# Decoder step on one core: the samples' outputs from the old recurrent state, the state's update moved behind the branches

## The chip, the core and the metric

The kernel runs on one core of a Trainium2 chip. The core has a matrix engine (TensorE, PE in the profile, with its weight loads as PEld), a vector engine (VectorE, DVE), a scalar engine (ScalarE, ACT), GpSimd (POOL) and SyncE (SP). Each takes its instructions in the order of its own queue and waits for others by semaphores. Transfers between the main memory and the on-chip memory are issued by SP, POOL and ACT and run on 16 DMA engines. TensorE writes into PSUM, a small accumulator memory that VectorE and ScalarE read.

The metric is the time of one execution on the device, in microseconds (us); less is better.

## What is computed

One layer of a decoder for a prompt of 256 tokens and, beside it, 8 samples with one new token each. The input projection feeds three parallel branches (a spatial gating, an HGRN2 recurrence with 8 heads of 128 x 128 state, a GLA recurrence with 4 heads of 128 x 256 state); their outputs are merged by gates, projected, and an MLP (2048 to 8192 and back) follows. All is in 32-bit floats. The part that matters here is the recurrence:

```python
"""S_t = diag(f_t) S_{t-1} + k_t v_t^T ; o_t = S_t^T q_t (per head)."""
o = einsum('bhts,bshv->bthv', att, vc) + einsum('bthd,bhdv->bthv', qc * exp(b), S)
S = exp(b_last)[..., None] * S + einsum('bshd,bshv->bhdv', kc * exp(b_last[:, None] - b), vc)
```

For a sample there is one step only: from the given state S, the decay f, the key k, the value v and the query q come the new state S' = diag(f) S + k vᵀ, which is an output of the kernel, and the output o = S'ᵀ q. The same output can be written with the old state: o = Sᵀ (f · q) + v (k · q).

## The kernel before

**The stream.** 256 prompt tokens and 8 samples stand together as 264 columns. Each weight block of 128 x 128 is split into a high part (`whi`, a cast on ScalarE, L109) and the rest (`wlo`, a subtraction on VectorE, L106), and each product takes three matmuls (L601 to L603) in which the columns pass. `granule` runs 24 such matmuls on a 512 KB piece of weights. `Stream` loads the pieces through SP into four `raw` buffers and splits them two pieces ahead, into six pairs of `whi` and `wlo`.

**Phases.** First the main input projection, in chunks; then the branch phase: `gla_group`, then for each of the three branches the gates' projection (`zin`) and the branch's own (`linear` with `w_branch`); then `w_out`; then the MLP in eight blocks, `up` of a block before `down` of the one ahead.

**Background work.** The branches' small work is written as generators. After each granule `background()` counts a tick (`now[0]`) and pumps two queues: `bg` (the mixers: transposes, decay levels, attention within the prompt) and `bs` (the samples' states), each with a rate per tick. `yield x` costs x of the rate, `yield READY` holds until the next tick, `yield` of a condition holds until it is true. `slot()` puts the small matmuls that have become ripe (levels, samples, the adaLN products of `Rounds`) into the stream, when something is due or has waited for some ticks.

**Who sets the order.** In the branch phase the order on PE and POOL is the program's own (`manual_schedule`), in the MLP phase that on PE alone. The instructions of the other engines are put in order by the framework's scheduler, which takes data and buffers into account; tiles with one name (`st`, `vbc`, `vt` and so on) share a fixed number of buffers.

**The samples' states before.** There are three groups: HGRN heads 0 to 3, heads 4 to 7 (state 128 x 128 a head), and GLA (128 x 256 a head). `mixer_r` brings the samples' values to rows and writes them to memory (`vs_d`, L1130); when the gates are done, `samples_r` (L1058) goes to `bs`. In 8 steps (16 for GLA) of one sample and 128 x 512 elements of state it loads the state into `st` (L1073, POOL) and the values, the same for all partitions, into `vbc` (L1079, POOL); multiplies by the decay on ScalarE (L1099, one instruction a head); adds value times key on VectorE (L1101); writes the new state out (L1102, POOL) and hands `st` to `samples`. `slot()` multiplies it with the query, masked so that each sample has its row (`qm`, L640), and VectorE adds the products to `os_` (L647, L103). At the end `os_` is normalised (L1111 to L1113), and `finish` (L1300) transposes it into the branch's columns. `st` has four buffers, `vbc` two; a further state is fetched only while at most one state is handed over and unread.

```python
for i in range(nh):
    S.activation(st[:, i, :], st[:, i, :], AF.Copy, scale=fs[:, h0 + i, b:b + 1])
for i in range(nh):
    V.scalar_tensor_tensor(st[:, i, :], v[:, i, :], k[:, h0 + i, NP + b:NP + b + 1], st[:, i, :], ALU.mult, ALU.add)
nc.gpsimd.dma_start(G.s_out(b, h0, nh), st)
```

Other lines that are spoken of: `srow` (L862, L865), the samples' rows in `sample_rows`; `G2`, a product of two vectors for the last norm, emitted ahead of the last `down`; the loads of `x_prompt` (L1406) behind the branches; L1220, the attention between the prompt's two halves, which needs `kd`; L1340 and L1342, the gating of a branch's product.

Of the kernel before, what the change touches and what calls it, by code (L numbers as in the profile page):

```python
# [10 lines left out]
AF = mybir.ActivationFunctionType  # L11
ALU = mybir.AluOpType
# [3 lines left out]
P = 128  # L16
D = 2048
KT = D // P
NP = 256
NS = 8  # L20
NT = NP + NS
# [16 lines left out]
ST_BUFS = 4  # L38
VB_BUFS = 2
# [8 lines left out]
READY = object()  # L48
SLOT_WAIT = 4
HELD_OWED = 1.0  # L50
LEVELS_HELD = 3
FETCHED = 3
AGE = 2
ADA_LAND = 4

# [2 lines left out]
def hybrid_step_kernel(  # L58
# [8 lines left out]
    nc = tc.nc  # L67
    V, S, T = nc.vector, nc.scalar, nc.tensor
# [29 lines left out]

    def mul(o, a, b):
        V.tensor_tensor(o, a, b, op=ALU.mult)  # L100

    def add(o, a, b):
        V.tensor_tensor(o, a, b, op=ALU.add)  # L103
# [14 lines left out]
    ident, ones, triu = cst[:, 0:128], cst[:, 128:256], cst[:, 256:384]  # L118
    rmask, delta = cst[:, 384:648], cst[:, 648:904]
# [29 lines left out]
    ps = sm()  # L149
# [205 lines left out]
    now = [0]  # L355
# [41 lines left out]
    bg, bs = Queue(), Queue()  # L397
# [98 lines left out]
    rate = [0.0, 0.0]  # L496
# [110 lines left out]
    levels, samples = [], []  # L607

    def slot():

        lv = [x for x in levels if x[0] + AGE <= now[0]][:2]
        if any(x[3] == 64 for x in lv):
            lv = lv[:1]
        sv = [x for x in samples if x[0] + AGE <= now[0]]
        del levels[:len(lv)]
        del samples[:len(sv)]
        pls, two = [], None
        for _, lhs, rhs, m, _ in lv:
            if m == 64:
                pl = sm([P, 8, 64])  # L620
            else:
                two = two or sm([P, 2, 8, 32])
                pl = two[:, len(pls)]
            pls.append(pl)
            n = max(m, 32)
            for h in range(4):
                for hf in range(2):
                    for b in range(4):
                        if m >= 32 and b // (n // 32) % 2:
                            continue  # L630
                        t0 = hf * P + b * 32
                        q0 = t0 if m < 32 else hf * P + b // (n // 32) * n + n
                        T.matmul(pl[32 * b:32 * b + 32, 2 * h + hf, :], lhs[:, h, t0:t0 + 32], rhs[:, h, q0:q0 + n], start=True, stop=True)  # L633
        if sv:
            G, qm, os_ = sv[0][1]
            nh = 512 // G.dv
            po = sm([P, G.dv])
            for h in range(4):
                for i, (_, _, b, sts) in enumerate(sv):
                    T.matmul(po[32 * h:32 * h + 32, :], qm[:, h, b, :], sts[h // nh][:, h % nh, :], start=i == 0, stop=i == len(sv) - 1)  # L640
        if rounds.due():
            rounds.steps()
        for pl, x in zip(pls, lv):
            x[4](pl)
        if sv:
            if sv[0][2] == 0:
                V.tensor_copy(os_, po)  # L647
            else:
                add(os_, os_, po)

    later = []

# [222 lines left out]
    def mixer_a():  # L875
# [6 lines left out]
        for gg in range(2):  # L882
            ps = sm()
# [5 lines left out]
        ps = sm()  # L889
# [3 lines left out]
        for v in vtk:  # L893
            st = tmp([P, 2, 6], "bst", 1)
# [11 lines left out]
            add(v, v, lnb)  # L906
            yield

        vs = tmp([P, 8, NS], "vsa", 1)
        w8 = tmp([P, 8, NS], "vsb", 1)  # L910
        r8 = tmp([P, NS], "vsr", 1)
        for i in range(2):
# [4 lines left out]
        ps = sum_partitions(w8, NS)  # L917
# [7 lines left out]
        ps = sum_partitions(w8, NS)  # L925
# [9 lines left out]
        ps = sm([P, P])  # L935
# [11 lines left out]
        for gp in range(4):  # L947
            ps = sm()
# [30 lines left out]

    att = const([P, 8, P], "att")  # L980
    nc.gpsimd.memset(att, 0.0)
    vs_d = dp.tile([3, 8 * NS, P], F32, tag="vs_d", name="vs_d")

    class Group:
# [73 lines left out]
    def samples_r(G):  # L1058

        dv = G.dv  # L1060
        nj, nh = dv // P, 512 // dv
        q, k, g = G.q, G.k, G.g
        fs = tmp([P, 4, NS], "fs")
        S.activation(fs, g[:, :, NP:NT], AF.Exp)
        qm = blk([P, 4, NS, 32])
        mul(qm, q[:, :, NP:NT].unsqueeze(3).to_broadcast([P, 4, NS, 32]),
            delta.rearrange("p (b c) -> p b c", b=NS).unsqueeze(1).to_broadcast([P, 4, NS, 32]))
        steps = [(b, h) for b in range(NS) for h in range(0, 4, nh)]
        ahead, vals = [], []

        def fetch(b, h):
            st = tmp([P, nh, dv], "st", ST_BUFS)
            nc.gpsimd.dma_start(st, G.s_in(b, h, nh))  # L1073
            ahead.append((st, now[0]))

        def values(b, h):
            v = tmp([P, 4, P], "vbc", VB_BUFS)
            r0 = 4 * nj * b + h * nj
            nc.gpsimd.dma_start(v, vs_d[G.i, r0:r0 + 4, :].partition_broadcast(P))  # L1079
            vals.append((v.rearrange("p (h j) v -> p h (j v)", h=nh), now[0]))  # L1080

        for s in steps[0:2]:
            fetch(*s)
            yield
        values(*steps[0])
        yield
        os_ = tmp([P, dv], f"os{G.i}", 1)
        sts = []
        for n, (b, h0) in enumerate(steps):
            if n + 2 < len(steps):  # L1090

                yield lambda: len(sts) + sum(len(x[3]) for x in samples) <= ST_BUFS - 3
                fetch(*steps[n + 2])
            if n + 1 < len(steps):
                values(*steps[n + 1])
            yield lambda: now[0] >= max(ahead[0][1] + FETCHED, vals[0][1] + FETCHED - 1)
            st, v = ahead.pop(0)[0], vals.pop(0)[0]
            for i in range(nh):
                S.activation(st[:, i, :], st[:, i, :], AF.Copy, scale=fs[:, h0 + i, b:b + 1])  # L1099
            for i in range(nh):  # L1100
                V.scalar_tensor_tensor(st[:, i, :], v[:, i, :], k[:, h0 + i, NP + b:NP + b + 1], st[:, i, :], ALU.mult, ALU.add)  # L1101
            nc.gpsimd.dma_start(G.s_out(b, h0, nh), st)  # L1102
            sts.append(st)
            if h0 + nh == 4:
                samples.append((now[0], (G, qm, os_), b, sts))
                sts = []
            yield
        yield lambda: not samples
        yield READY
        ss, rr = tmp([P, 1], "sss", 1), tmp([P, 1], "srr", 1)  # L1110
        S.activation(tmp([P, dv], "vt"), os_, AF.Square, accum_out=ss)  # L1111
        rstd_small(ss, 1.0 / dv, rr)
        S.activation(os_, os_, AF.Copy, scale=rr)  # L1113
        G.os = os_
        yield

    def mixer_r(G):
# [172 lines left out]
                yield 0.6  # L1290
        G.o = o

    def finish(i):
        bg.drain(gens[i])
        G = Gs[i]
        while not hasattr(G, "os"):
            bs.drain(bs.g[0])
        for j in range(G.dv // P):
            ps = sm([P, P])
            T.transpose(ps, G.os[:, j * P:(j + 1) * P], ident)  # L1300
            V.tensor_copy(G.o[j][:, :, NP:NT], ps.rearrange("p (h c) -> p h c", h=4)[:, :, 0:NS])

    gens, Gs = [], []
# [101 lines left out]
        for hf in range(2):  # L1405
            nc.gpsimd.dma_start(x1[t][hf], x_prompt[0, t * P:(t + 1) * P, hf * 1024:(hf + 1) * 1024])  # L1406
    sqacc = tmp([P, NT], "a32", 1)
    gs = tmp([P, KT, NS], "gs", 1)

    def gated(m, src, Gv):  # L1410

# [62 lines left out]
    for m in range(7):  # L1474
        if m in PRE_AT:
            n = N_PRE // len(PRE_AT)
# [77 lines left out]
    ps = sm([P, 2, 14, NS])  # L1554
# [16 lines left out]
    ps = sm([P, 2 + NS])  # L1571
# [35 lines left out]
    q = tmp([P, 2 + NS], "rr", 1)  # L1607
# [116 lines left out]
    def up(f, zs=()):  # L1724
        ah, al = [], []
        for m in range(FB // CW):
            z = zs[m] if m < len(zs) else linear(w_mlp_up[0], 0, KT, f * FB + m * CW, CW, h2H, h2L)
            rl = tmp([P, 2, NT], "vt")
            S.activation(rl, z, AF.Relu)  # L1729
            if m % 2 == 0:  # L1730
                ah.append(blk(dt=F32R))
                al.append(blk(dt=F32R))
            a, b = pair(ah[-1], m % 2), pair(al[-1], m % 2)
            sq = tmp([P, 2, NT], "gt")
            S.activation(a, rl, AF.Square)  # L1735
            mul(sq, rl, rl)
            sub(b, sq, a.bitcast(F32))
        return tiles(ah), tiles(al)
# [31 lines left out]
    order = tc.manual_schedule(engines={mybir.EngineType.PE})  # L1770
    order.__enter__()
    pend = up(0, zs)
    for f in range(NFB):
        nxt = up(f + 1) if f + 1 < NFB else None
        if f == NFB - 1:
            rounds.drain()
            mul(G2, mod[:, 5 * KT:6 * KT, :], gpost2T.unsqueeze(2).to_broadcast([P, KT, NC]))
            yt = [[blk([P, 1024]) for _ in range(2)] for _ in range(2)]
        g = down(f, *pend)
        pend = nxt  # L1780
# [89 lines left out]
```

## Time and profile before

| What | Value |
|---|---|
| Median of 3 runs | 1937.15 us (1937.14 to 1942.04) |
| Profiled execution | 1936.48 us |
| Its span in the trace | 1934.7 us |
| TensorE busy | 1900.5 us |
| VectorE busy | 1191.7 us |
| ScalarE busy | 996.9 us |
| DMA traffic | 442.06 MB, 228 GB/s on the mean |
| Loads of states (`st`) | 32 of 256 KB |
| Loads of values (`vbc`) | 32 of 256 KB |
| Writes of states | 32 of 256 KB |

Line numbers (L1101) are those of the kernel before. A group's row gives line, engine and operation, what it writes and reads, the shapes and the count, then its busy time, the mean length of one in ns, and the idle time of its engine just ahead of it with what ended most of that. A row of a timeline gives start, length, engine, line and operation, and in brackets the idle time ahead and its releaser. A row of windows gives a stretch, its length, the busy time of PE, PEld, DVE, ACT and POOL (with instructions), then the clock that TensorE was granted, the share of the DMA engines in use and GB/s. A row that begins with a line and has "min/median/max" in ns gives also the first and last start in us.

### The profile page before, as it was taken

How to read it: one execution, taken by the hardware profiler on the slowest of the kernel's cores; microseconds unless marked ns; L12 is line 12 of the kernel's file. 1: busy time of each engine (PE TensorE's matmuls, PEld its weight loads, DVE VectorE, ACT ScalarE, POOL GpSimd, SP SyncE). 2: the span in 40 equal slices, each digit the busy share in tenths (PEclk: the TensorE clock that was granted, in tenths of full speed). 3: DMA queues.
4: the chain of work that ended last, by engine and by line, in shares of the span. 5: the costliest groups of instructions: out<-in, count | busy, mean ns of one | idle time of the engine just before them, and what ended most of it. 6: DMA issues, size and time to landing. Idle time of an engine off the chain costs nothing.

```text
span 1934.7 us, 42322 instructions
## 1 busy us (share of the span) xinstructions
PE 1900.5 (98%) x17092; PEld 1811.2 (94%) x17092; DVE 1191.7 (62%) x2129; ACT 996.9 (52%) x1812; POOL 87.7 (5%) x144
## 2 busy tenths in 40 slices
PE   7999999998999999999999999999999999999998
PEld 5989999998999998999999999999999999999997
DVE  5666567685577695565555667545555555555666
ACT  4444354664666765544444566454444545454544
POOL 1000000001101112200000010000000000000000
PEclk9999999999999999999999999999999999999999
DMA  9986696777588678987777846776655556565563
GB/s 325 349 319 236 226 307 206 226 254 252 184 269 278 221 260 277 309 264 251 251 252 231 304 143 193 230 239 188 183 178 183 182 179 184 176 184 179 181 183 102
DMA packets 339380, 442.06 MB, mean 228 GB/s; under 512 B 14930, under 2 KB 281024, under 8 KB 339184
## 3 DMA queue, kind: packets, MB, share of 16 engines
q1 hardware_dynamic: 329120, 409.62, 65.6%
q0 software_dynamic: 8992, 28.48, 4.6%
q8 instruction: 134, 2.20, 0.4%
q10 hardware_dynamic: 1072, 1.25, 0.2%
q14 instruction: 62, 0.51, 0.1%
HBM read 427.60 MB, written 11.70 MB: 227 GB/s over the span
## 4 chain that ended last, share of the span: by engine, by line
PE 94%; DVE 2%; DMA 2%; ACT 1%; issue 1%; POOL 0%; SPq 0%; DVEq 0%; ACTq 0%
PE mm L601 29%; PE mm L602 28%; PE mm L603 28%; PE ada L341 3%; PE ada L273 2%; DMA vbc<-vs_d 1%; PE sm L633 1%; DVE wlo L106 1%; PE sm L845 1%; PE sm L640 0%; DMA st<-in_state_gla_dram 0%; DMA b<-in_x_prompt_dram 0%; DVE b L103 0%; DMA b<-in_w_ada_dram 0%; ACT b L109 0%
## 5 line engine op out<-in xcount | busy, mean ns | idle before, releaser
L601 PE MATMUL mm<-b,whi 128*128 128x264 f32 x4592 | 1318.1, 287 | 5.7 <-DVE b L103 2.9
L602 PE MATMUL mm<-b,whi 128*128 128x264 f32 x4592 | 1307.7, 285 | 1.4 <-DVE b L106 1.2
L603 PE MATMUL mm<-b,wlo 128*128 128x264 f32 x4592 | 1305.1, 284 | 3.1 <-DVE wlo L106 2.6
L106 DVE TENSOR_TENSOR wlo<-raw,whi 128x512 fp32r<-128x512 f32 x1136 | 770.3, 689 | 498.0 <-ACT whi L109 495.4
L109 ACT CAST whi<-raw 128x512 fp32r<-128x512 f32 x1132 | 692.3, 618 | 726.9 <-PE mm L602 648.2
L601 PEld LDWEIGHTS mm<-b,whi 128*128 128x128 f32 x4592 | 865.4, 188 | 49.2 <-issue 24.7
L603 PEld LDWEIGHTS mm<-b,wlo 128*128 128x128 f32 x4592 | 865.5, 188 | 3.7 <-DVE wlo L106 3.7
L602 PEld LDWEIGHTS mm<-b,whi 128*128 128x128 f32 x4592 | 865.5, 188 | 2.4 <-DVE b L106 1.3
L103 DVE TENSOR_TENSOR b<-b,mm 128x528 f32<-128x528 f32 (+1 forms) x137 | 95.7, 700 | 98.2 <-PE mm L603 98.2
L1101 DVE SCALAR_TENSOR_TENSOR st<-vbc,b,st 128x128 f32<-128x128 f32 (+1 forms) x96 | 34.2, 391 | 54.7 <-DMA vbc<-vs_d 49.8
L1099 ACT ACTIVATE st<-st,fs 128x128 f32<-128x128 f32 (+1 forms) x96 | 37.0, 430 | 58.7 <-DMA st<-in_state_hgrn_dram 32.5
L273 PE MATMUL ada<-b,cT 128*32 128x256 f32 (+1 forms) x640 | 34.7, 354 | 6.9 <-DMA b<-in_w_ada_dram 6.8
L341 PE MATMUL ada<-araw,cT 128*32 128x512 f32 x296 | 39.9, 601 | 0.0
L273 PEld LDWEIGHTS ada<-b,cT 128*32 128x32 f32 x640 | 17.8, 112 | 18.8 <-ACT b L234 6.1
L100 DVE TENSOR_TENSOR b<-b,b 128x512 f32<-128x512 f32 (+1 forms) x47 | 34.1, 742 | 1.4 <-ACT b L1209 0.9
L1102 POOL DMA_DIRECT2D out_dram<-st x32 | 23.5, 735 | 156.4 <-DVE st L1101 155.6
L341 PE MATMUL ada<-b,cT 128*32 128x512 f32 x216 | 25.8, 593 | 0.0
L106 DVE TENSOR_TENSOR b<-gt,b 128x528 fp32r<-128x528 f32 x32 | 22.7, 708 | 3.6 <-ACT whi L109 0.5
L106 DVE TENSOR_TENSOR b<-b 128x1024 f32<-128x1024 f32 (+1 forms) x24 | 24.3, 1018 | 0.0
L100 DVE TENSOR_TENSOR gt<-vt 128x528 f32<-128x528 f32 x32 | 22.5, 702 | 0.9 <-ACT vt L1729 0.9
L1735 ACT ACTIVATE b<-vt 128x528 fp32r<-128x528 f32 x32 | 20.7, 647 | 1.0
L341 PEld LDWEIGHTS ada<-b,cT 128*32 128x32 f32 x216 | 6.9, 110 | 15.1 <-issue 14.6
(385 smaller groups left out, 882.6 us busy)
## 6 DMA issues: line engine op xcount, KB each, us to landing
raw<-in_w_in_dram SPq DMA_DIRECT2D x232, 512.0 KB, 4.6
raw<-in_w_mlp_up_dram SPq DMA_DIRECT2D x128, 512.0 KB, 3.7
raw<-in_w_mlp_down_dram SPq DMA_DIRECT2D x128, 512.0 KB, 3.6
b<-in_w_ada_dram SPq DMA_DIRECT2D x102, 512.0 KB, 6.3
araw<-in_w_ada_dram SPq DMA_DIRECT2D x74, 512.0 KB, 5.4
raw<-in_w_branch_dram SPq DMA_DIRECT2D x48, 512.0 KB, 4.3
raw<-in_w_out_dram SPq DMA_DIRECT2D x32, 512.0 KB, 4.2
b<-in_w_ada_dram SPq DMA_DIRECT2D x32, 256.0 KB, 6.5
```

Source lines behind the costliest of these rows:

```text
L100: V.tensor_tensor(o, a, b, op=ALU.mult)
L103: V.tensor_tensor(o, a, b, op=ALU.add)
L106: V.tensor_tensor(o, a, b, op=ALU.subtract)
L109: S.copy(hi, src)
L273: T.matmul(acc[32 * j:32 * j + 32, 0:n], cT[:, k, :], w[:, n * j:n * j + n], start=k == 0, stop=k == KT - 1)
L341: T.matmul(self.acc[32 * j:32 * j + 32, :], cT[:, k, :], ws[j // 2][:, j % 2 * 512:j % 2 * 512 + 512], start=k == 0, stop=k == KT - 1)
L601: T.matmul(o, a, xh(k + j), start=first and j == 0, stop=False)
L602: T.matmul(o, a, xl(k + j), start=False, stop=False)
L603: T.matmul(o, b, xh(k + j), start=False, stop=last and j == n - 1)
L1099: S.activation(st[:, i, :], st[:, i, :], AF.Copy, scale=fs[:, h0 + i, b:b + 1])
L1101: V.scalar_tensor_tensor(st[:, i, :], v[:, i, :], k[:, h0 + i, NP + b:NP + b + 1], st[:, i, :], ALU.mult, ALU.add)
L1102: nc.gpsimd.dma_start(G.s_out(b, h0, nh), st)
```

## The change

In `samples_r` the state is not updated any more. The old state is loaded and handed to `slot()` as it is; the masked query is multiplied by the decay first (`qf`). The second term, value times (key · query), goes into `os_` ahead of the products: the samples' values are copied to a padded tile, transposed by PE (one transpose for a group of HGRN, two for GLA), and scaled by key · query, for which PE multiplies `pads` (by then k times q) with a column of ones. Loads now alternate over six buffers (every third takes a `vbc` buffer), and up to three states may wait for PE. Decay and key of each group are kept in a new tile, `kept`.

A new generator, `states()`, goes to `bs` when the first block of `up` has been issued, at a rate of 0.4 a tick. It walks over all 32 steps, loads state and values again, and does the multiplication on ScalarE, the addition on VectorE and the write that `samples_r` did. The names of three small tiles change so that they share buffers.

```diff
-FETCHED = 3
+FETCHED = 4
+UPDATE_RATE = 0.4
...
-            if sv[0][2] == 0:
-                V.tensor_copy(os_, po)
-            else:
-                add(os_, os_, po)
+            add(os_, os_, po)
...
+    kept = const([P, 3, 2, 4 * NS], "kept")
...
-        fs = tmp([P, 4, NS], "fs")
+        fs, ks = (kept[:, G.i, c].rearrange("p (h b) -> p h b", h=4) for c in range(2))
         S.activation(fs, g[:, :, NP:NT], AF.Exp)
+        V.tensor_copy(ks, k[:, :, NP:NT])
+        yield
...
         def fetch(b, h):
-            st = tmp([P, nh, dv], "st", ST_BUFS)
+            odd = fetched[0] % 3 == 2
+            fetched[0] += 1
+            st = tmp([P, nh, dv], "vbc" if odd else "st", VB_BUFS if odd else ST_BUFS)
             nc.gpsimd.dma_start(st, G.s_in(b, h, nh))
...
+        pads = tmp([P, 4, 32], "xsn", 1)
+        nc.gpsimd.memset(pads, 0.0)
+        for j in range(nj):
+            for i, b in enumerate(G.v):
+                V.tensor_copy(pads[:, i * nh:(i + 1) * nh, 0:NS], b[:, j::nj, NP:NT])
+            yield READY
+            yield READY
+            ps = sm([P, P])
+            T.transpose(ps, pads.rearrange("p h b -> p (h b)"), ident)
+            S.copy(os_[:, j * P:(j + 1) * P], ps)
+            yield
+        qf = tmp([P, 4, NS], "fs")
+        mul(pads[:, :, 0:NS], q[:, :, NP:NT], ks)
+        mul(qf, q[:, :, NP:NT], fs)
         yield
...
+        yield READY
+        ps = sm([P, 8])
+        T.matmul(ps[:, 0:1], pads.rearrange("p h b -> p (h b)"), ones[:, 0:1], start=True, stop=True)
+        kq = tmp([P, 1], "sss", 1)
+        V.tensor_copy(kq, ps[:, 0:1])
+        yield
+        S.activation(os_, os_, AF.Copy, scale=kq)
+        yield
...
-                yield lambda: len(sts) + sum(len(x[3]) for x in samples) <= ST_BUFS - 3
+                yield lambda: len(sts) + sum(len(x[3]) for x in samples) <= ST_BUFS - 1
                 fetch(*steps[n + 2])
...
-            for i in range(nh):
-                S.activation(st[:, i, :], st[:, i, :], AF.Copy, scale=fs[:, h0 + i, b:b + 1])
-            for i in range(nh):
-                V.scalar_tensor_tensor(st[:, i, :], v[:, i, :], k[:, h0 + i, NP + b:NP + b + 1], st[:, i, :], ALU.mult, ALU.add)
-            nc.gpsimd.dma_start(G.s_out(b, h0, nh), st)
-            sts.append(st)
+            yield lambda: now[0] >= ahead[0][1] + FETCHED
+            sts.append(ahead.pop(0)[0])
...
-            yield
+            yield 0.5
...
+    def states():
+
+        todo = [(G, b, h) for G in Gs for b in range(NS) for h in range(0, 4, 512 // G.dv)]
+        ahead = []
+
+        def fetch(G, b, h):
+            nj, nh = G.dv // P, 512 // G.dv
+            st, v = tmp([P, nh, G.dv], "st", ST_BUFS), tmp([P, 4, P], "vbc", VB_BUFS)
+            nc.gpsimd.dma_start(st, G.s_in(b, h, nh))
+            r0 = 4 * nj * b + h * nj
+            nc.gpsimd.dma_start(v, vs_d[G.i, r0:r0 + 4, :].partition_broadcast(P))
+            ahead.append((st, v.rearrange("p (h j) v -> p h (j v)", h=nh), now[0]))
+
+        fetch(*todo[0])
+        yield
+        for n, (G, b, h) in enumerate(todo):
+            if n + 1 < len(todo):
+                fetch(*todo[n + 1])
+                yield 0.5
+            yield lambda: now[0] >= ahead[0][2] + FETCHED
+            st, v = ahead.pop(0)[0:2]
+            nh = 512 // G.dv
+            for i in range(nh):
+                f, k = (kept[:, G.i, c, (h + i) * NS + b:(h + i) * NS + b + 1] for c in range(2))
+                S.activation(st[:, i, :], st[:, i, :], AF.Copy, scale=f)
+                V.scalar_tensor_tensor(st[:, i, :], v[:, i, :], k, st[:, i, :], ALU.mult, ALU.add)
+                if i % 2:
+                    yield 0.5
+            nc.gpsimd.dma_start(G.s_out(b, h, nh), st)
+            yield
...
     pend = up(0, zs)
+    bs.g.append(states())
+    rate[:] = (0.0, UPDATE_RATE)
...
             rounds.drain()
+            assert not bs.g
```

More of the change, by code (lines that the diff above doesn't have):

```diff
@@ L907, in mixer_a @@
             yield
-        vs = tmp([P, 8, NS], "vsa", 1)
+        vs = tmp([P, 8, NS], "os1", 1)
         w8 = tmp([P, 8, NS], "vsb", 1)
@@ L1062, in samples_r @@
         q, k, g = G.q, G.k, G.g
-        fs = tmp([P, 4, NS], "fs")
+        fs, ks = (kept[:, G.i, c].rearrange("p (h b) -> p h b", h=4) for c in range(2))
         S.activation(fs, g[:, :, NP:NT], AF.Exp)
-        qm = blk([P, 4, NS, 32])
-        mul(qm, q[:, :, NP:NT].unsqueeze(3).to_broadcast([P, 4, NS, 32]),
-            delta.rearrange("p (b c) -> p b c", b=NS).unsqueeze(1).to_broadcast([P, 4, NS, 32]))
+        V.tensor_copy(ks, k[:, :, NP:NT])
+        yield
         steps = [(b, h) for b in range(NS) for h in range(0, 4, nh)]
-        ahead, vals = [], []
+        ahead, fetched = [], [0]
@@ L1071, in fetch @@
         def fetch(b, h):
-            st = tmp([P, nh, dv], "st", ST_BUFS)
+            odd = fetched[0] % 3 == 2
+            fetched[0] += 1
+            st = tmp([P, nh, dv], "vbc" if odd else "st", VB_BUFS if odd else ST_BUFS)
             nc.gpsimd.dma_start(st, G.s_in(b, h, nh))
             ahead.append((st, now[0]))
[L1076 to L1080, printed above, removed]
@@ L1082, in samples_r @@
         for s in steps[0:2]:
             fetch(*s)
+        os_ = tmp([P, dv], f"os{G.i}", 1)
+        pads = tmp([P, 4, 32], "xsn", 1)
[8 more added lines that the diff above has]
+            S.copy(os_[:, j * P:(j + 1) * P], ps)
@@ L1084, in samples_r @@
             yield
-        values(*steps[0])
+        qf = tmp([P, 4, NS], "fs")
+        mul(pads[:, :, 0:NS], q[:, :, NP:NT], ks)
+        mul(qf, q[:, :, NP:NT], fs)
         yield
-        os_ = tmp([P, dv], f"os{G.i}", 1)
+        qm = blk([P, 4, NS, 32])
+        mul(qm, qf.unsqueeze(3).to_broadcast([P, 4, NS, 32]),
+            delta.rearrange("p (b c) -> p b c", b=NS).unsqueeze(1).to_broadcast([P, 4, NS, 32]))
+        yield READY
+        ps = sm([P, 8])
+        T.matmul(ps[:, 0:1], pads.rearrange("p h b -> p (h b)"), ones[:, 0:1], start=True, stop=True)
@@ L1090, in samples_r @@
             if n + 2 < len(steps):
-                yield lambda: len(sts) + sum(len(x[3]) for x in samples) <= ST_BUFS - 3
+                yield lambda: len(sts) + sum(len(x[3]) for x in samples) <= ST_BUFS - 1
                 fetch(*steps[n + 2])
[L1094 to L1097, printed above, removed]
-            for i in range(nh):
-                S.activation(st[:, i, :], st[:, i, :], AF.Copy, scale=fs[:, h0 + i, b:b + 1])
-            for i in range(nh):
-                V.scalar_tensor_tensor(st[:, i, :], v[:, i, :], k[:, h0 + i, NP + b:NP + b + 1], st[:, i, :], ALU.mult, ALU.add)
-            nc.gpsimd.dma_start(G.s_out(b, h0, nh), st)
-            sts.append(st)
+            yield lambda: now[0] >= ahead[0][1] + FETCHED
+            sts.append(ahead.pop(0)[0])
             if h0 + nh == 4:
@@ L1407, in hybrid_step_kernel @@
     sqacc = tmp([P, NT], "a32", 1)
-    gs = tmp([P, KT, NS], "gs", 1)
+    gs = tmp([P, KT, NS], "os0", 1)
     def gated(m, src, Gv):
```

## The prediction

> **What bounds the kernel now.** I read the page's head, the chain, what TensorE (PE) waits for, and then the windows.
>
> ```profile
> span 1934.7 us, 42322 instructions
> PE 1900.5 (98%) x17092; PEld 1811.2 (94%) x17092; DVE 1191.7 (62%) x2129; ACT 996.9 (52%) x1812; POOL 87.7 (5%) x144
> PE 94%; DVE 2%; DMA 2%; ACT 1%; issue 1%; POOL 0%; SPq 0%; DVEq 0%; ACTq 0%
> ```
>
> PE is busy 98% of the span and 94% of the chain is PE. Only two things can move the time: PE's own work, and the places where PE stands. Between 320 and 520 us PE's waits are these two (us in total, times, longest), in the 350 us that follow only the next two:
>
> ```profile
> PE sm L1220 <- DVE b L100: 3.8, 1, 3.8
> PE mm L603 <- DVE wlo L106: 1.9, 1, 1.9
> ...
> PE mm L603 <- issue: 0.5, 1, 0.5
> PE mm L603 <- DVE wlo L106: 0.2, 1, 0.2
> ```
>
> The timelines of VectorE (DVE) and PE (start, length; in brackets the idle time before and its releaser) show where they come from:
>
> ```profile
> 454.92 0.61 DVE L1101 SCALAR_TENSOR_TENSOR st<-vbc,b,st 128x128 f32<-128x128 f32 x2 [7.71 <-DMA vbc<-vs_d]
> 456.81 0.39 PE L603 MATMUL mm<-b,wlo 128*128 128x264 f32 x1 [1.91 <-DVE wlo L106]
> 471.51 0.88 DVE L1101 SCALAR_TENSOR_TENSOR st<-vbc,b,st 128x128 f32<-128x128 f32 x3 [1.26 <-DMA vbc<-vs_d]
> 477.75 0.49 PE L1220 MATMUL sm<-b,b 128*128 128x128 f32 x2 [3.84 <-DVE b L100]
> ```
>
> DVE works in queue order. At 447 us the state update (L1101) is at its head and waits 7.71 us for the broadcast values, `vbc`; the weight halves `wlo` behind it come late, and PE stands 1.91 us. Its backlog, with more update instructions and another wait, makes `kd` late at 477 us: 3.84 us. Both gaps are followed by matmuls at about half the clock (window, its length, busy PE, PEld, DVE, ACT, POOL; granted clock, DMA share, GB/s):
>
> ```profile
> 458.00:462.00 4.00, 3.97 (x20) 3.67 (x19) 3.71 (x7) 3.46 (x10) 0.00 (x0) 0.57 0.55 141
> 478.00:482.00 4.00, 4.00 (x23) 4.00 (x23) 0.30 (x1) 1.14 (x2) 0.00 (x0) 0.59 0.93 300
> ```
>
> That costs 4 x 0.43 = 1.7 and 4 x 0.41 = 1.6 us. Updates of the samples' states thus hold PE up by 1.9 + 3.8 + 1.7 + 1.6 = **9.1 us**, all in group 0.
>
> The Trainium skill's page "TensorE: Matmul & The Clock Gate" (What's actually happening) has the clock halve after at least one idle window of about 3.4 us; here a gap of 1.91 us was enough. By the page the first gap would cost 1.9 us and the gain would be 7.4 us; the windows decide for 9.1.
>
> **The change, part by part.**
>
> *The update leaves the branch phase.* PE no longer waits for ScalarE (ACT), DVE or `vbc`; it reads the old state as it lands. A slot comes at least 4 + 2 background ticks after the fetch is emitted; a tick is 24 matmuls. With 2305 matmuls in 280 us (a window quoted below) that is 2.9 us, so 17 us against a landing of 11.3 at most (next rows). I put PE's wait for these loads at nothing. Both stalls go: -9.1. The least that I allow is -5, if the chain to L1220 stays late for other reasons; the most is -9.8, with the 0.5 and 0.2 above.
>
> *New PE work*: 4 transposes of the samples' values and 3 products with a column of ones, in some 7 visits. The nearest rows are a visit with two transposes:
>
> ```profile
> 668.65 0.28 PE L603 MATMUL mm<-b,wlo 128*128 128x264 f32 x1
> 668.77 0.38 PE L1300 MATMUL sm<-cst,os 128*128 128x128 f32 x2
> 668.91 0.37 PE L601 MATMUL mm<-b,whi 128*128 128x264 f32 x1
> 669.11 0.28 PE L602 MATMUL mm<-b,whi 128*128 128x264 f32 x1
> ```
>
> From L603 to L602 are 0.46 us, where two steps of the stream (0.12 each, 668.65 to 668.77) take 0.24: 0.22 a visit, 7 x 0.22 = **+1.5 us** (0.7 if visits fall together, 3 if each stands alone). The small copies and products on DVE and ACT replace 32 updates there, and the new memset on POOL stands behind two fetches that POOL issues well ahead; I cost them at nothing. Should POOL be late, DVE waits about 2 us, which the update's longer waits without a PE stall (below) show to be covered.
>
> *The update elsewhere*: 32 steps, each with a second load of the state, the broadcast `vbc`, 96 ACT and 96 DVE instructions in all, and the write. The issue times on POOL, in ns (min/median/max), and the landings:
>
> ```profile
> L1099 ACT ACTIVATE st<-st,fs 128x128 f32<-128x128 f32 (+1 forms) x96 | 37.0, 430 | 58.7 <-DMA st<-in_state_hgrn_dram 32.5
> L1101 DVE SCALAR_TENSOR_TENSOR st<-vbc,b,st 128x128 f32<-128x128 f32 (+1 forms) x96 | 34.2, 391 | 54.7 <-DMA vbc<-vs_d 49.8
> L1102 POOL DMA_DIRECT2D out_dram<-st x32: 712/742/764, 404.7 to 836.6; - x32
> L1073 POOL DMA_DIRECT2D st<-in_state_gla_dram x16: 707/722/732, 665.5 to 821.7; - x16
> L1079 POOL DMA_DIRECT2D vbc<-vs_d x32: 549/562/809, 374.7 to 830.8; - x32
> DMA to landing us min/median/max: 3.7/6.5/11.3
> ```
>
> A step costs 34.2/32 = 1.07 us of DVE, 37.0/32 = 1.16 of ACT and 0.74 + 0.72 + 0.56 = 2.0 of POOL. Spread over the MLP phase (0.4 a tick, 2 to 2.5 a step: one step in 5 to 6 ticks, 16 us) this would cost nothing: DVE is at 164/280 = 58% there, DMA at 0.60.
>
> ```profile
> 1600.00:1880.00 280.00, 280.00 (x2305) 280.00 (x2305) 163.62 (x244) 132.59 (x218) 0.00 (x0) 1.00 0.60 181
> ```
>
> **But will it be spread?** In that phase only PE's order is fixed by hand. What the scheduler does with instructions of other engines can be read from early starters:
>
> ```profile
> L100 DVE TENSOR_TENSOR G<-mod,vec x2: 302/304/306, 559.5 to 1340.6; 128x144 f32<-128x144 f32 x2
> L1419 DVE TENSOR_SCALAR gt<-b,G x8: 347/348/354, 1877.7 to 1921.3; 128x256 f32<-128x256 f32 x8
> L862 DVE COPY srow<-b x4: 190/192/200, 346.1 to 530.5; 128x32 f32<-128x32 f32 x4
> L865 PE MATMUL sm<-cst,srow x3: 271/272/272, 369.0 to 662.8; 128*128 128x128 f32 x3
> L1406 POOL DMA_DIRECT2D b<-in_x_prompt_dram x4: 528/546/569, 1011.6 to 1029.5; - x4
> L1342 DVE SCALAR_TENSOR_TENSOR gt<-gt,mm x16: 693/704/705, 689.3 to 1046.3; 128x528 f32<-128x528 f32 x16
> ```
>
> The product for `G2` is emitted ahead of the last `down` block, a few us before its first use at 1877.7; it ran at 1340.6, when its input was there. The copies into `srow` are emitted just before their transposes (662.8 the last); the last ran at 530.5. Both went up, by 130 and 530 us, to their data. The loads of `x_prompt` came early too, but not at the start: their tiles took their turn in the pool. The pacing by ticks fixes PE's order alone. `states()` hands PE nothing, so its loads start when the `st` tiles, in their turn, come free after the last samples' matmuls, and each step then follows as fast as two `vbc` buffers allow:
>
> ```profile
> L640 PE MATMUL sm<-st,b x192: 269/279/404, 424.9 to 845.3; 128*32 128x128 f32 x128, 128*32 128x256 f32 x64
> 802.63 0.72 POOL L1073 DMA_DIRECT2D st<-in_state_gla_dram x1 [8.07 <-PE sm L640]
> 801.68 0.62 ACT L109 CAST whi<-raw 128x512 fp32r<-128x512 f32 x1 [0.84 <-PE mm L602]
> 809.14 0.91 ACT L1099 ACTIVATE st<-st,fs 128x256 f32<-128x256 f32 x2 [6.83 <-DMA st<-in_state_gla_dram]
> 40.00:100.00 60.00, 60.00 (x647) 54.99 (x646) 38.45 (x66) 25.85 (x44) 0.00 (x0) 1.00 0.97 342
> 840.00:1050.00 210.00, 210.00 (x1734) 198.32 (x1733) 116.68 (x186) 95.16 (x154) 2.18 (x4) 1.00 0.77 251
> ```
>
> So I expect the 32 updates from about 845 us, beside the third branch. The load issued at 802.63 landed at 809.1, yet its consumer stands in ACT's queue right behind the cast of 801.68, one cast (1.5 us) later than the slot: the order counts on loads that land in about 2 us. The order is therefore as dense as the engines allow: DVE is idle 1 - 117/210 = 44% there, so a step takes 1.07/0.44 = 2.4 us of planned time, in which PE does 2.4 us of work. On the chip a step takes longer. By latency, two in flight: (2.0 + 6.5 + 1.07)/2 = 4.8 us with the median landing, 3.4 with the shortest. By traffic: three transfers of 0.262 MB plus PE's weights for 2.4 us at 251 GB/s (0.60 MB) make 1.39 MB, at the 342 GB/s of a stretch with DMA at 0.97: 4.1 us. I take 4.1, between the latency ends. PE loses (4.1 - 2.4) x 32 = 54 us, less one cover of about 7 us (the 6.83 us wait above brought no PE stall worth naming): **+47 us**. The ends: 3.4 gives 32 - 7 = 25, 4.8 gives 77 - 7 = 70.
>
> The sum: the profiled execution took 1936.48 us, 1.8 above its span and 0.7 below the median of the runs. 1936.5 - 9.1 + 1.5 + 47 = 1975.9; with the 0.7, 1976.6, say **1976**.
>
> **Rivals.**
>
> *A, the update does stay in the MLP phase.* If tiles of one pool are handed out in program order whatever their name, the `st` tiles wait their turn behind the `vt` and `gt` tiles of `up`, which PE paces. For it: the turn that the `x_prompt` tiles took. Against it: those share one name with what held them, and tiles of another pool did not hold them: they came before the last accumulator ahead of them was read (L1342, 1046.3). Then 1937.2 - 9.1 + 1.5 = 1929.6, **faster**. It decides as soon as a step takes over 4.8 us of planned time, the time of one by latency: all landings are then hidden.
>
> *B, dense, but landings are short.* The shortest landing of a state load was 3.0 us:
>
> ```profile
> DMA to landing us min/median/max: 3.0/5.7/11.3
> ```
>
> A step then takes (2.0 + 3.0 + 1.07)/2 = 3.0 us, PE loses 0.6 x 32 - 7 = 12, and the time is 1942 (1932 to 1955). For it: a standing PE asks for fewer weights. Against it: medians of 5.7 and 6.5 at spacings wider than here. The Trainium skill's page "DMA: Bandwidth & Descriptors" (Anatomy of one DMA, SWDGE path) fits 2.0 us plus bytes over 436 GB/s, 2.6 us for such a load; by that, an estimate, the step takes 2.8 us and 6 us are lost after the cover, 1936. No landing of these loads in the trace was that short.
>
> *C, the stalls are replaced*: spread or not, a new wait in the branch phase (a transpose or product whose copy on DVE or ACT is late) takes back what L1220 gives. One such gap with its slow clock is 3.8 + 1.6 = 5.4 us: 1935. For it: three groups, seven new points where PE needs something from DVE. Against it: ready-waits of one or two ticks ahead of each.
>
> *D, spread, but DVE waits for `vbc` in the MLP phase.* `down` frees an accumulator every two granules, 5.8 us, so waits over about 6 us stall PE, at 1.9 + 1.7 to 3.8 + 1.6 us each: with four of them 1929.6 + 18 = 1948. Against it: DMA at 0.60 and 16 us between steps.
>
> **How the numbers follow.** Forecast (dense, 1955 to 2007) 0.47; A 0.25; B 0.12; C 0.09; D 0.07. About 0.3% (5.8 us) is what a measurement can tell from no change. Faster: A's 0.22 and 0.02 of B and C, 0.24. Same: A 0.03, B 0.04, C 0.07, D 0.02, in all 0.16. Slower: 0.60. The range goes from A's 1928 to 2005, where the upper latency end (1976.6 + 70 - 47 = 2000) and some slow clock behind the gaps lie; below and above it about 0.15 are left out. The forecast's own range is 1955 to 2005.
>
> **What would show it.** Dense: the update's ACT and DVE lines start near 845 us and end before 1000; DVE waits there for `vbc` tens of us in total; PE waits for `wlo` and `whi`, its busy share falls, and DMA rises above 0.9 in these slices. Spread: the same lines run from about 1200 to 1740 us and PE has no gap there. In either case the gaps at 455 and 474 us are gone, no L1101-like line stands before 800 us, and PE has 7 short visits more. I am wrong if the update starts late, or if it starts at 845 us and PE still does not stand; and in the branch part, if PE waits for `st` loads.

## The result and the profile after

The kernel after the change takes 1995.0 us (median of 5 runs, 1994.37 to 1996.86), the one before 1937.15 us on the same chip (5 runs): ratio 1.030, 95% interval [1.029, 1.031]. It is slower by 58 us, where the forecast was 1976 us in a range of 1928 to 2005. The profiled execution took 1996.86 us, 2.1 us above its span.

The page of the kernel after: its head, then TensorE's (PE's) busy time and granted clock in 40 slices of 50 us, and the share of each engine in the chain that ended last.

```profile
span 1994.8 us, 42421 instructions
PE 1922.0 (96%) x17102; PEld 1826.6 (92%) x17102; DVE 1198.8 (60%) x2143; ACT 1001.0 (50%) x1819; POOL 111.3 (6%) x179
PE   7999999999999999876899999999999999999998
...
PEclk9999999999999999988999999999999999999999
...
PE 80%; issue 9%; DMA 6%; DVE 2%; POOL 1%; ACT 1%; SPq 0%; DVEq 0%; ACTq 0%; POOLq 0%
```

PE's share of the chain fell from 94% to 80%. Its busy digits drop in slices 17 to 20, 800 to 1000 us, its clock in two of these; elsewhere only the first and the last slice are below 9. PE is busy for 21.5 us more than before with ten instructions more: a part of the loss is PE itself running slower. The rows of the `st` tiles say what runs in those slices (ns min/median/max, first and last start in us):

```profile
L1326 ACT ACTIVATE st<-st,kept x96: 384/398/512, 803.1 to 964.9; 128x128 f32<-128x128 f32 x64, 128x256 f32<-128x256 f32 x32
L1327 DVE SCALAR_TENSOR_TENSOR st<-vbc,kept,st x96: 343/348/485, 804.3 to 979.0; 128x128 f32<-128x128 f32 x64, 128x256 f32<-128x256 f32 x32
```

So all 32 steps of the update, emitted in the MLP phase, ran at 803 to 979 us, 5.5 us a step, beside the third branch. What the engines waited for between 785 and 990 us (us in total, times, longest): PE, then VectorE (DVE), ScalarE (ACT) and GpSimd (POOL):

```profile
PE mm L604 <- DVE wlo L107: 22.7, 17, 4.8
PE mm L602 <- ACT whi L110: 19.1, 8, 9.6
PE mm L602 <- ACT gt L1373: 2.4, 2, 2.0
...
DVE wlo L107 <- ACT whi L110: 39.2, 23, 5.0
DVE st L1327 <- DMA vbc<-vs_d: 33.0, 10, 5.5
...
ACT st L1326 <- DMA st<-in_state_hgrn_dram: 30.8, 7, 8.3
ACT st L1326 <- DMA st<-in_state_gla_dram: 23.4, 8, 6.7
...
POOL st L1310 <- DMA out_dram<-st: 57.6, 24, 5.9
```

An ACT or DVE that stands for a load of the update has the casts and subtractions of the weight stream behind it; PE then has no `whi` or `wlo`. PE's three lines add up to 44.2 us. The windows (length; busy PE, PEld, DVE, ACT, POOL with instructions; granted clock, DMA share, GB/s), first over the whole stretch, then its worst part, then the places of the two old stalls; below them the first and the last of these stretches in the kernel before:

```profile
785.00:985.00 200.00, 155.57 (x1094) 140.78 (x1093) 100.38 (x219) 89.23 (x201) 64.59 (x96) 0.88 0.86 277
...
920.00:960.00 40.00, 23.95 (x146) 22.78 (x145) 19.80 (x40) 16.82 (x33) 15.24 (x23) 0.74 0.90 301
...
455.00:482.00 27.00, 27.00 (x300) 25.68 (x299) 15.39 (x32) 13.35 (x25) 0.00 (x0) 1.00 0.63 184
```

```profile
785.00:985.00 200.00, 199.79 (x1657) 187.01 (x1653) 111.58 (x192) 95.53 (x168) 13.97 (x21) 1.00 0.83 271
...
455.00:482.00 27.00, 21.33 (x185) 19.83 (x186) 20.58 (x41) 14.57 (x31) 4.84 (x7) 0.88 0.82 263
```

In 200 us PE stood for 44.4 us, and the clock of 0.88 took another 0.12 x 200 = 24 us: 68 us lost. The count of matmuls says the same: 1094 where the kernel before ran 1657, and 563 at 200/1657 = 0.121 us are 68 us. The two stalls of before are gone (27.00 of 27 us busy at full clock), which gave back 5.7 us of idle time and 0.12 x 27 = 3.2 us of clock, less the time of the new PE work. With some 8 us for that, 68 - 8 = 60 is the difference of the spans (1994.8 - 1934.7).

### The profile page after: what moved, and what is told of

Same layout as the page of the kernel before. It is cut to its first block, busy times and chain, and to the rows that moved or that the text cites. A ratio compares the mean times of both kernels' runs of the same rounds, so it can differ in the third digit from the quotient of the medians.

```text
span 1994.8 us, 42421 instructions
## 1 busy us (share of the span) xinstructions
PE 1922.0 (96%) x17102; PEld 1826.6 (92%) x17102; DVE 1198.8 (60%) x2143; ACT 1001.0 (50%) x1819; POOL 111.3 (6%) x179
## 4 chain that ended last, share of the span: by engine, by line
PE 80%; issue 9%; DMA 6%; DVE 2%; POOL 1%; ACT 1%; SPq 0%; DVEq 0%; ACTq 0%; POOLq 0%
PE mm L602 24%; PE mm L603 24%; PE mm L604 24%; DMA out_dram<-st 3%; PE ada L342 2%; PE ada L274 1%; DMA st<-in_state_hgrn_dram 1%; DMA vbc<-vs_d 1%; DMA st<-in_state_gla_dram 1%; DVE wlo L107 1%; DMA raw<-in_w_in_dram 1%; POOL st L1310 1%; PE sm L634 1%; PE sm L843 1%; DMA b<-in_x_prompt_dram 0%
## 5 line engine op out<-in xcount | busy, mean ns | idle before, releaser
L1326 ACT ACTIVATE st<-st,kept 128x128 f32<-128x128 f32 (+1 forms) x96 | 36.2, 428 | 95.8 <-DMA st<-in_state_hgrn_dram 30.8
L1327 DVE SCALAR_TENSOR_TENSOR st<-vbc,kept,st 128x128 f32<-128x128 f32 (+1 forms) x96 | 33.7, 392 | 64.8 <-DMA vbc<-vs_d 33.0
```

The source lines that it names most:

```text
L1326: S.activation(st[:, i, :], st[:, i, :], AF.Copy, scale=f)
L1327: V.scalar_tensor_tensor(st[:, i, :], v[:, i, :], k, st[:, i, :], ALU.mult, ALU.add)
```

## The experiments

All ratios are to the kernel before, which took 1935.1 to 1936.8 us (medians of 7 to 16 runs) beside these kernels. Lines are those of the kernel named.

**1. The branch phase alone.** The generator `states()` isn't started: the new states are not computed and not written.

```diff
-    bs.g.append(states())
-    rate[:] = (0.0, UPDATE_RATE)
```

> Leaves out the second pass over the states (no states(), so the samples' new states are not written); the branch phase is that of the changed kernel. Theory (the early, dense update is the whole loss, and the branch part alone gains 9.1 us less 1.5 us of new PE work): about 1930 us (1928 to 1932), no gap of PE between 380 and 1000 us. Rival (the new transposes, products and loads of the branch phase cost something themselves): 1935 us or more, with gaps of PE before 800 us.

1927.83 us, ratio 0.9955 [0.9937, 0.9972]. This is the floor: what the change gains in the branch phase, 8.9 us here, without the update. From 785 to 985 us PE is busy for all of the 200 us. All losses below are counted from it; the kernel after loses 67 us.

**2. The rate.**

```diff
-UPDATE_RATE = 0.4
+UPDATE_RATE = 1.0
```

> UPDATE_RATE 1.0 in place of 0.4 and nothing else. Theory (the rate sets only the place in the program, not the order on POOL, ACT and DVE): update lines again from about 800 to 980 us, 1985 to 2005 us. Rival (the rate sets the density of the update): the update 2.5 times as dense, a loss 2 times as large, above 2030 us, or the update at another place.

1995.64 us, 1.0305 [1.0283, 1.0328], with the update at 802 to 976 us. At 2.5 times the rate it stays where it was: the pacing by ticks has no hold on it.

**3. A data dependence that holds the loads back.** The tiles get a value that the MLP phase makes just then; the load overwrites it, and so can't start earlier.

```diff
 st, v = tmp([P, nh, G.dv], "st", ST_BUFS), tmp([P, 4, P], "vbc", VB_BUFS)
+V.tensor_copy(st[:, 0, 0:1], newest[0])
+V.tensor_copy(v[:, 0, 0:1], newest[0])
...
+            newest[0] = sq[:, 0, 0:1]
...
+            newest[0] = dst[:, 0, 0:1]
```

> The changed kernel with two one-column copies on DVE ahead of each pair of loads of states(), from the newest result of up or down into the tiles to be loaded, so that a load cannot start before PE has come that far. Same traffic and same ACT and DVE work as the changed kernel. Theory (the update costs nothing where it is spread): 1929 to 1932 us, update lines from about 1200 to 1720 us, no gap of PE above 1 us in the MLP phase. Rival (25 MB more and 192 instructions cost PE time wherever they stand, by traffic or by waits of DVE for the broadcast values): above 1940 us.

1929.73 us, 0.9963 [0.9950, 0.9975]: 7 us faster than the kernel before, with every output. What ACT (for the update, whole run) and PE (1200 to 1740 us) waited for:

```profile
ACT st L1329 <- DMA st<-in_state_gla_dram: 61.9, 16, 7.1
ACT st L1329 <- DMA st<-in_state_hgrn_dram: 42.5, 15, 5.3
...
PE mm L604 <- DVE wlo L107: 0.9, 2, 0.5
PE mm L602 <- DVE b L104: 0.7, 1, 0.7
```

At 16 us a step (1205 to 1722 us) ACT still stands 3.4 us for each load (104.4 us in 31 waits), and it costs PE next to nothing: its two rows, 1.6 us, are all its waits there.

**4. Which part of the dense update costs.** Three kernels, each with a part of `states()` left out: the two instructions on ACT and DVE (loads and write remain; the states written are the old ones), the write (the states are not written), or the load of `vbc` and the addition (the states are only decayed).

```diff
-                S.activation(st[:, i, :], st[:, i, :], AF.Copy, scale=f)
-                V.scalar_tensor_tensor(st[:, i, :], v[:, i, :], k, st[:, i, :], ALU.mult, ALU.add)
```

> states() loads and stores as in the changed kernel but leaves out the multiplication and the addition, so the old states are written out unchanged. Theory (PE stands because ACT and DVE wait in queue order for loads that their order counts on earlier): under 1945 us, with gaps of PE only where weights land late. Rival (the traffic itself delays the weights): 1975 us or more.

```diff
-            nc.gpsimd.dma_start(G.s_out(b, h, nh), st)
```

> The changed kernel without the stores of states() (the samples' new states are computed and not written). In the changed kernel POOL waited 57.6 us for stores to land before it could load into the same buffer, a wait that the prediction's step of 4.1 us did not have. Theory (that wait makes the real step 5.5 us): without it a step takes (0.72 + 0.56 + 6.3 + 1.07)/2 = 4.3 us, and the loss shrinks to about half, 1950 to 1970 us. Rival (the two vbc buffers alone set the step): 1985 us or more.

```diff
-            nc.gpsimd.dma_start(v, vs_d[G.i, r0:r0 + 4, :].partition_broadcast(P))
...
-                V.scalar_tensor_tensor(st[:, i, :], v[:, i, :], k, st[:, i, :], ALU.mult, ALU.add)
```

> The changed kernel with the addition of value times key and the loads of vbc left out of states(): load, decay on ACT, store. Theory (both queues stall, ACT for the states and DVE for vbc): DVE's waits and their share go, ACT's stay, 1945 to 1970 us. Rival (DVE alone makes the gaps): under 1940 us; rival (ACT alone): 1985 us or more.

| What remains of the update | us | ratio | lost from the floor |
|---|---|---|---|
| loads and write | 1944.37 | 1.0035 [1.0017, 1.0053] | 17 |
| load of the state, decay, write | 1966.60 | 1.0149 [1.0122, 1.0176] | 39 |
| all but the write | 1984.35 | 1.0240 [1.0205, 1.0275] | 57 |
| all | 1995.0 | 1.030 [1.029, 1.031] | 67 |

Traffic by itself, at the highest rate of any run here, loses a quarter of it. Windows of the kernel with loads and write alone (the whole update, then 100 us of it), then of the one without the write:

```profile
785.00:945.00 160.00, 149.90 (x1189) 137.61 (x1189) 74.33 (x128) 65.28 (x115) 64.89 (x97) 0.98 1.01 365
800.00:900.00 100.00, 96.72 (x794) 91.33 (x793) 45.52 (x81) 38.32 (x66) 44.01 (x65) 1.00 1.03 370
```

```profile
785.00:945.00 160.00, 125.29 (x903) 112.30 (x902) 84.86 (x197) 79.95 (x183) 40.85 (x64) 0.93 0.83 262
```

In the same 160 us PE is 94% busy at 365 GB/s where no ACT or DVE instruction waits for a load of the update, and 78% busy at 262 GB/s where they do. Without the write I had expected at most 1970 us: a step did become shorter (800.7 to 928.5 us, 4.0 us), but the loss fell by 11 us only (two runs, 1980.4 and 1988.3 us). So neither the bytes nor the turn of the buffers is the larger part. By elimination the instructions that wait are; what exactly is wrong with them this does not say.

**5. The same density in the MLP phase.** If it is the place beside the third branch that costs, an update that is dense but later should be cheaper. The gate of experiment 3 is tied to the newest `wlo` instead, with rate 1.0 and a hold of one tick, or rate 2.0 and none. (The hold is the number of ticks between emitting a load and emitting its use, `FETCHED` in the kernel after.)

```diff
-UPDATE_RATE = 0.4
+UPDATE_RATE = 1.0
...
+                newest[0] = lo[:, 0, 0:1].bitcast(F32)
...
-            yield lambda: now[0] >= ahead[0][2] + FETCHED
+            yield lambda: now[0] >= ahead[0][2] + 1
```

> Loads of states() gated as in e2, by the newest wlo tile, at rate 1.0 and a hold of 1 tick: one step in 2 to 2.5 ticks, 5.8 to 7.3 us. Theory (PE loses only where the planned step is shorter than the real one, 5.5 us at most): 1929 to 1934 us. Rival (any spacing well below that of e2 costs): above 1940 us.

> As e6, at rate 2.0 with no hold: one step in 1 to 1.25 ticks, 2.9 to 3.6 us, as dense as the changed kernel had planned it, but in the MLP phase with 180 GB/s of weights in place of 250. Theory (density decides, not the place): PE stands again, 1950 to 1990 us, update lines over 100 to 170 us. Rival (the place decides: the branch phase was short of DMA, the MLP phase is not): under 1937 us.

2030.23 us (1.0478 [1.0457, 1.0498]) and 1999.93 us (1.0320 [1.0303, 1.0338]). The first is a miss by 100 us, and worse than the denser one, which is itself 10 us above the range expected of it. So the place doesn't decide, and neither does a theory in which a longer time between steps always helps. The kernel of the first, around one step (timelines of ACT, DVE, POOL and PE: start, length; in brackets the idle time ahead and its releaser):

```profile
1306.93 0.62 ACT L110 CAST whi<-raw 128x512 fp32r<-128x512 f32 x1
1313.40 0.69 ACT L1329 ACTIVATE st<-st,kept 128x128 f32<-128x128 f32 x2 [5.85 <-DMA st<-in_state_hgrn_dram]
1314.00 0.60 ACT L110 CAST whi<-raw 128x512 fp32r<-128x512 f32 x1
...
1307.61 0.68 DVE L107 TENSOR_TENSOR wlo<-raw,whi 128x512 fp32r<-128x512 f32 x1
1314.06 0.61 DVE L1330 SCALAR_TENSOR_TENSOR st<-vbc,kept,st 128x128 f32<-128x128 f32 x2 [5.77 <-DMA vbc<-vs_d]
...
1307.92 0.75 POOL L1313 DMA_DIRECT2D st<-in_state_hgrn_dram  x1
...
1314.66 0.39 PE L603 MATMUL mm<-b,whi 128*128 128x264 f32 x1 [2.91 <-ACT whi L110]
```

POOL issues the load at 1307.92. ACT has its use next in its queue after the cast of 1306.93 and stands until 1313.40, with the next cast behind it; PE gets that cast's `whi` 2.91 us late. The order of the queue has almost no time between a load and its use.

**6. The same density, another lead.** This gave a new theory: what costs is the **lead**, the work that stands in the queue between a load and its use. Two kernels with the gate of experiment 5, rate 1.0 and a hold of four ticks. In one of them the decay column that ACT multiplies with is written again when the hold is over, from the newest `wlo` times 0 plus the column:

```diff
+            late = tmp([P, 4], "late", 1)
+            V.scalar_tensor_tensor(late[:, 0:nh], newest[0][:, 0:nh], 0.0, kept[:, G.i, 0, h * NS + b:(h + nh - 1) * NS + b + 1:NS], ALU.mult, ALU.add)
...
-                f, k = (kept[:, G.i, c, (h + i) * NS + b:(h + i) * NS + b + 1] for c in range(2))
+                f, k = late[:, i:i + 1], kept[:, G.i, 1, (h + i) * NS + b:(h + i) * NS + b + 1]
```

> As in e6_gated_2 the loads are tied to the newest wlo, and the order of ScalarE has the same density: 4.5 casts of 1.46 us from one step to the next, 6.6 us. New: the decay column that ScalarE multiplies with is rewritten (into a small tile, from the newest wlo times 0 plus the column) by VectorE four ticks after the load is emitted, so that no activation can stand in ScalarE's queue ahead of that point. Lead theory (what costs is a use that stands one cast behind its load): 1928 to 1942 us, PE waits for wlo and whi under 8 us in total over the whole run, the loads are still waited for on ScalarE by less than 30 us in total. Density theory (32 steps at this spacing cost what they cost in e6_gated_2, by traffic or by engine time): 1985 to 2030 us.

> The control of e9_factor_gated: the same gate on the loads, the same rate 1.0 and hold of four ticks, 4.5 casts from one step to the next in ScalarE's order, but the decay column is not rewritten, so that the use may go up to right behind its load. Lead theory: 1975 to 2035 us, tens of us of ScalarE waiting for st loads and of PE waiting for whi. Rival (the hold of four ticks instead of one is what helps): under 1945 us, as e9_factor_gated.

| Kernel | us | ratio | casts per step on ACT | `wlo` between gate and use on DVE |
|---|---|---|---|---|
| experiment 5, rate 1.0 | 2030.23 | 1.0478 [1.0457, 1.0498] | 4.5 | 2.3 |
| hold of four ticks | 2034.70 | 1.0500 [1.0475, 1.0525] | 4.5 | 2.3 |
| the same, column rewritten | 1928.70 | 0.9963 [0.9948, 0.9978] | 4.5 | 9.0 |

The three have the same work in the same density, 4.5 casts of 1.46 us (280 us for 192 casts) or 6.6 us a step; the third has one small instruction more in each step. With 2.3 subtractions (3.4 us) between the gate of a load and its use the update loses 102 and 107 us; with 9.0 (13 us) it loses 1 us. On ACT, 0.2, 0.3 and 7.9 casts start between the issue of a load and its use, in the order of the table. The window of the kernel with the hold alone, then its waits of ScalarE in it:

```profile
1200.00:1540.00 340.00, 275.21 (x1903) 257.92 (x1902) 151.55 (x345) 132.34 (x281) 64.76 (x96) 0.89 0.66 211
```

```profile
ACT st L1329 <- DMA st<-in_state_hgrn_dram: 83.9, 13, 9.6
ACT st L1329 <- DMA st<-in_state_gla_dram: 75.9, 12, 7.2
```

The same window of the one with the column rewritten, in which PE has no wait at all:

```profile
1200.00:1540.00 340.00, 340.00 (x2789) 332.71 (x2788) 224.80 (x470) 191.59 (x364) 64.78 (x96) 1.00 0.83 271
```

Nor do the loads land sooner. Median us from issue to landing of `vbc` in that window, in the kernel of experiment 5 and in the one with the column rewritten:

```profile
vbc<-vs_d POOLq DMA_DIRECT2D x32, 256.0 KB, 5.9
```

```profile
vbc<-vs_d POOLq DMA_DIRECT2D x32, 256.0 KB, 6.4
```

They take a little longer where nothing is lost.

**7. The smallest repair.** The kernel after, rate 0.4 and hold of four ticks, with the rewritten column alone; the loads are free to go early.

> The kernel after the change (rate 0.4, hold of four ticks, loads not tied to anything) with one instruction more in a step: VectorE rewrites the decay column from the newest wlo, as in e9_factor_gated. The four st tiles and two vbc tiles then bound how far the loads can run ahead. Lead theory: 1926 to 1934 us, no wait of PE for wlo or whi between 785 and 990 us beyond 2 us in total, ScalarE waits for st loads under 20 us in total. Rival (the loads must be held back too, or they collide with the weights near 800 us): 1940 us or more.

1928.53 us (1927.17 to 1930.61), 0.9962 [0.9948, 0.9975]. The rows of the use and of the loads of the HGRN states, then the window that had lost 68 us:

```profile
L1329 ACT ACTIVATE st<-st,late x96: 385/398/511, 1216.4 to 1730.1; 128x128 f32<-128x128 f32 x64, 128x256 f32<-128x256 f32 x32
...
L1311 POOL DMA_DIRECT2D st<-in_state_hgrn_dram x16: 747/747/764, 794.9 to 1430.4; - x16
```

```profile
785.00:985.00 200.00, 200.00 (x1658) 188.13 (x1657) 108.71 (x174) 91.61 (x153) 4.10 (x6) 1.00 0.79 256
```

The first loads still go at 795 us, fill the four tiles and wait there for 400 us, which harms nothing. One instruction of at most 4 columns a step, 32 in all, takes the change from 58 us slower to 7 us faster than before. It does as well as the kernel with both gates and the one of experiment 3 (1928.5 to 1929.7 us), and within a microsecond or two of the floor.

## Why the prediction came out as it did

**The branch phase (-9.1 + 1.5): right.** Both gaps and their slow clock are gone, and no wait of PE on a load of the old state appears. The term is 7.6 us; three kernels whose update costs next to nothing are 6.4 to 7.0 us faster than the kernel before beside them, and the one without update 8.9 us.

**The new PE work: right as far as it can be seen.** PE has ten instructions more (17102 against 17092) where the prediction counted seven: the four transposes, and six records for the three products with a column of ones. Their price of about a microsecond can't be read from these times.

**The update pulled forward: right.** It ran at 803 to 979 us; I had said from about 845 to before 1000. The start was 42 us off: the `st` tiles came free earlier, with the last samples' matmuls at 812 us and not at 845. The signs named for the dense case are there but for one: `vbc` was waited for by tens of us and PE waited for `wlo` and `whi`, but DMA reached 0.90 in the stretches of 40 us and did not rise above it.

**The price of the dense update (+47): the mis-sized term.** The idle time came out as 44 us, but the clock behind the gaps took 24 us more, and this was not in the sum; I had charged it to the two old gaps and then left it out for the new ones, apart from a remark at the upper end of the range. With it the sum is 1929 + 68 = 1997. The two lengths behind the 47 were also both short: a step took 5.5 us and not 4.1, because a new load waits for the landing of an old write from the same tile (57.6 us of POOL; without the write it took 4.0), a wait that the working lacked; and the order had 3.4 us of PE's work in a step, not 2.4 (PE ran 900 matmuls from 803 to 980 us, at the 0.121 us of the kernel before 109 us, by 32). The difference of the two is 2.1 us a step against 1.7, or 67 us for 32 steps. The cover of 7 us that the prediction took off does not show.

**By traffic: the wrong reason for a near number.** That 47 lies close to the 44 us of idle time is luck. I took 4.1 us for a step because so many bytes need so long at 342 GB/s. Experiment 4 carries the same bytes at 365 GB/s and loses 17 us. The larger part is ACT and DVE standing for a load with the weight stream behind them. The prediction had read exactly this from the cast of 801.68 and the use of 809.14 ("the order counts on loads that land in about 2 us"), and then used it for the density alone.

**Rival A: its case did not come, its price was right, its rule was wrong.** The scheduler did not keep the update in the MLP phase; where a data dependence does so at 16 us a step, the time is 1928.5 to 1929.7 us, as priced (1929.6). But the rule that it decides "as soon as a step takes over 4.8 us of planned time", because "all landings are then hidden", fell: two kernels with 6.6 us of planned time lost over 100 us. A landing is hidden by what stands between the load and its use, not by the time from one step to the next. With a short lead the spacing has another role. In the kernel of experiment 5 ACT stood for (85.3 + 76.2 + 36.5)/32 = 6.2 us a step, these rows being its waits for the update:

```profile
ACT st L1329 <- DMA st<-in_state_hgrn_dram: 85.3, 14, 8.1
ACT st L1329 <- DMA st<-in_state_gla_dram: 76.2, 12, 8.0
...
ACT st L1329 <- issue: 36.5, 6, 7.4
```

Between two such stops the busier of the two engines, DVE, which is 66% busy (224.80 of 340 us in the undisturbed window above), catches up 0.34 x 6.6 = 2.2 us, so that the order falls back by some 4 us; PE lost (2030.2 - 1927.8)/32 = 3.2 us a step. At 16 us and 58% it catches up 6.7 us, more than the 3.4 us that ACT stood in experiment 3. The kernel at rate 2.0 comes out of it too: there ACT stood 105.8 us for the update in all its rows, 3.3 us a step, and the order has 2.2 casts or 3.2 us a step, in which 1.1 us are caught up; that leaves 2.2 us, and PE lost (1999.9 - 1927.8)/32 = 2.3. This is an estimate that fits three spacings, not a test: none between 6.6 and 16 us was run.

**Rivals B, C and D: did not come.** In the kernel after, the loads issued between 785 and 985 us took 5.8 to 6.4 us at the median to land, not 3.0. The fit on the Trainium skill's page "DMA: Bandwidth & Descriptors" (Anatomy of one DMA, SWDGE path), 2.6 us by the prediction's estimate, is not borne out for loads beside this weight stream. The branch phase got no new gap: from 380 to 785 us PE was busy for all of the 405 us. And waits in the MLP phase at 16 us a step stalled nothing.

Not tried: an update at 3.4 us a step with a long lead. The traffic of experiment 4 suggests that it would lose something there too.

## What to carry to other kernels

When work is handed to a scheduler, ask two things of its order: how early it can go, and how much stands in the queue between a load and its use. Where the order has less time there than a landing takes, each use stops its engine with everything behind it, and spreading the steps helps only if the engine can catch up before the next one. A small instruction that ties the use (not the load) to a value made a few microseconds later sets that lead; and the price of a gap on PE has the slow clock behind it as a term of its own.

## What the runs showed of the hardware

In these traces many short gaps held the clock down. In the kernel with the hold alone PE stood for 65 us of 340 us, in 40 gaps of at most 5.5 us, and was granted 0.89, so the clock took another 37 us, more than half as much as the gaps. And the transfers of a core can go above the 342 GB/s that I had taken for full: 370 GB/s over 100 us, at a share of 1.03, with the granted clock at 1.00.
